# A decoder layer on one core: rows ahead of x, a later gate load, a first block by parts, rows used one place behind their loads, and wide products of ones

## The chip, the cores and the metric

The kernel runs on one core of a Trainium2 chip. The metric is the device time of one execution in microseconds (us). The core's engines run their own instruction streams: PE (TensorE, matmuls and transposes, with weight loads shown apart as PEld), DVE (VectorE), ACT (ScalarE), POOL (GpSimd) and SP (SyncE, which here only issues loads). Sixteen DMA engines move what SP, ACT and POOL issue.

## The reference

One hybrid decoder layer in float32, for 256 rows of width 2048. A conditioning vector `c` gives six rows of shifts, scales and gates by one matrix-vector product; the normalised and modulated `x` goes through a projection, two kinds of mixing heads, an output projection, and then a second normalisation and a gated feed-forward network.

```
c_act = silu(c)
mod = (c_act @ w_mod + b_mod)[:, None, :]            # w_mod: 2048 x 12288
sh_m, sc_m, g_m, sh_f, sc_f, g_f = split(mod, 6)
h = rmsnorm(x, mix_pre_w) * (1 + sc_m) + sh_m
proj = h @ w_in                                       # 2048 x 6160
cb, cc, cx, q, k, v, r, a_lr = split(proj, ...)       # a_lr: the last 16 columns
y_conv = cb * causal_dwconv3(cc * cx, conv_w)
log_a = log_sigmoid(a_lr @ gate_w2 + gate_b) / 16     # gate of the linear attention
o = rmsnorm(gla_chunked(q, k, v, log_a), gla_norm_w) * silu(r)
x = x + g_m * rmsnorm(concat(y_conv, o) @ w_out, mix_post_w)
h = rmsnorm(x, ffn_pre_w) * (1 + sc_f) + sh_f
u = causal_dwconv3(h @ w_up, ffn_conv_w)
g, val = split(u, 2)
x = x + g_f * rmsnorm((silu(g) * val) @ w_down, ffn_post_w)
```

## The kernel before

**Products in parts.** Each float32 matrix product is made of three faster ones: a weight tile is cast to a rounded type by ACT (`high`, line 140, tile `wh`), the remainder is taken by DVE (`low`, line 145, tile `wl`), and the activations are split likewise (`act_high`, `act_low`, line 380). A block adds high x high, high x low and low x high (lines 501 to 503).

**Units.** Work on PE is a list of units in a fixed order. A unit has `prep` (issue its weight load on SP, cast it on ACT), `low` (subtract on DVE), `mm` (its matmuls) and lists of other work at four places (`early`, `pre`, `mid`, `late`). `drive` walks the list: in unit i it runs `early`, then `prep` of unit i+2 and `low` of unit i+1, then `pre`, the matmuls, `mid` and `late`. All engines receive their instructions in this written order; what makes them wait is data and free buffers. Loaded tiles rotate through six `raw` buffers, `wh` and `wl` through three each, and most other tiles through twenty `big` buffers of one size (`slot`).

**Chunks.** The depth of the first projection (16 tiles of 128) is cut into `CHUNKS` of 2, 4, 5 and 5 tiles, with 12, 12, 16 and 18 units; then come 16 units of the output projection (`owait`), and the feed-forward part. Units of the first two chunks have four output tiles, those of the third three. A unit of the first chunk has 4 x 2 x 3 matmuls of 256 columns, one of the second 4 x 4 x 3, one of the third 3 x 5 x 3. In the list, unit 0 starts the first chunk, unit 12 the second, unit 24 the third, unit 40 the fourth.

**Modulation rows.** A chunk can only begin when its shift and scale are known. `mod_steps` computes them in 16 steps: step j loads the rows of `w_mod` that belong to c's j-th elements (SP) and adds them, times `c_act[:, j]`, to an accumulator over 128 partitions (DVE, line 136). For the chunks after the first these steps are spread over the `early` and `mid` places of the units given by `MODS`: units 0 to 9 for the second chunk, 10 to 20 for the third, 21 to 30 for the fourth, 31 to 43 for the gate row of the mixer, 44 to 67 for the first half of the feed-forward modulation. Then `mod_columns` sums the accumulator over the partitions and turns it into columns, by products with a matrix of ones of which 2 columns are used (line 282). Two units before a chunk ends (`LEAD`), the products for the next one stand in `early`, and in `late` the columns and the modulation of the activations (line 367); one unit later come the low parts and the products with the 16 gate columns `alr_w` (line 439), whose sum is taken in the next chunk's first unit (lines 447 and 449).

**The start.** For the first chunk the 16 steps stand ahead of everything. Four rows come in one load up to row 11, then two and two; the two halves of x (`load_x`) are issued after steps 0 and 8, and the norm of each (`NLD`, after steps 3 and 14) is computed as soon as it is written: squares on ACT (line 348), a sum on DVE (line 316), a root on ACT (line 318), a reciprocal on DVE (line 339), then the scaling of x, the first two tiles' columns on DVE (line 1028) and the rest on ACT (lines 1029 and 1030). After the rows SP loads `alr_w`, 16 columns of a wide matrix (line 1031). PE transposes x (line 361), sums the accumulator (line 282), and when the columns are there and the activations are modulated, cast and subtracted, it makes the gate products and begins unit 0. `drive` issues the first `prep`, `low` and second `prep` itself.

Of the kernel before, what the change touches and what calls it, by code (L numbers as in the profile page):

```python
# [14 lines left out]
P = 128  # L15
D = 2048
T = 256
# [19 lines left out]
XLD = (0, 8)  # L37
NLD = (3, 14)
# [3 lines left out]
MODS = (10, 21, 31, 44, 68)  # L42
# [7 lines left out]
NHF = 3  # L50

# [52 lines left out]
def layer_kernel(ctx: ExitStack, tc, x, c, w_mod, b_mod, mix_pre_w, mix_post_w, w_in, conv_w, gate_w2, gate_b,  # L104
# [47 lines left out]
    nc.scalar.activation(c_act, c_sb, AF.Silu)  # L152

# [3 lines left out]
    def mod_steps(s0, n, a, w, nj, first=False):  # L157

        accs, cur = [], {}

        def step(j):
            if j == 0:
                acc = cur["acc"] = (slot([P, n, w]) if n * w <= 1024 else
                                    wts.tile([P, n, w], F32, tag="macc", name=nm("macc"), bufs=2))
                accs.extend(acc[:, s, :] for s in range(n))
                if first:
                    cur["b"] = slot([1, n, w])
                    nc.gpsimd.dma_start(cur["b"], b_mod_v[:, s0:s0 + n, a:a + w])
                else:
                    nc.gpsimd.memset(acc, 0.0)  # L170
                    nc.gpsimd.dma_start(acc[0:1, :, :], b_mod_v[:, s0:s0 + n, a:a + w])
# [8 lines left out]
            src, cj = cur["r"][:, j % m, :, :], c_act[:, j:j + 1]  # L180
            if first and j == 0:
                nc.vector.tensor_scalar_mul(cur["acc"], src, cj)
            else:
                stt(cur["acc"], src, cj, cur["acc"])
            if first and j == 3:
                nc.vector.tensor_add(cur["acc"][0:1], cur["acc"][0:1], cur["b"])

        return accs, [lambda j=j: step(j) for j in range(KT)]

    accs0, steps0 = mod_steps(0, 2, 0, CHUNKS[0] * P, 4 if CHUNKS[0] < 3 else 2, True)  # L190

    ident = col(P, "ident")
    nc.scalar.dma_start(ident, ident_in)
# [3 lines left out]
    nc.scalar.copy(ones_r, ones)  # L197
    eps_t = col(1, "eps_t")
    nc.gpsimd.memset(eps_t, EPS)
# [69 lines left out]
    def mod_columns(accs, n, pre, tagname):  # L269

        ash = const.tile([P, 2 * n], F32, tag=tagname, name=nm("ash"))
        st = {}

        def products(tiles=None):
            r = ones if len(accs) == 2 else ones_r
            if "ps" not in st:
                st["ps"] = bank([P, 2 * n, 2])
            for o in (range(2 * n) if tiles is None else tiles):
                cs = slice((o % n) * P, (o % n + 1) * P)
                terms = (accs[o // n],) if len(accs) == 2 else accs[2 + o // n]  # L280
                for j, t in enumerate(terms):
                    nc.tensor.matmul(st["ps"][:, o, :], t[:, cs], r[:, 0:2], start=j == 0, stop=j == len(terms) - 1)  # L282

        def columns():
            nc.vector.tensor_copy(ash[:, :n], st["ps"][:, :n, 0])
            stt(ash[:, n:], st["ps"][:, n:, 0], 1.0, pre, ALU.add, ALU.mult)
# [134 lines left out]
    def modulate_chunk(ci, ash, early=None):  # L421
# [3 lines left out]

        def first():
            for kts in pairs(k0, k1):
                ps = early.pop(0) if early else turn_norm(xs, kts)
                hf = hf0[:, kts[0]:kts[-1] + 1, :] if ci == 0 else hf_tile()
# [5 lines left out]
        def second():  # L435
            ps = bank([P, T])
            for kts, hf, parts in kept:
                for i, k in enumerate(kts):
                    nc.tensor.matmul(ps[:16, :], alr_w[:, k, :], hf[:, i, :], start=(k == k0), stop=(k == k1 - 1))  # L439
                if parts:  # L440
                    act_low(*parts)
            kept.append(ps)

        def third():
            ps = kept.pop()
            if ci == 0:
                nc.vector.tensor_copy(alr[:16, :], ps[:16, :])
            else:
                nc.vector.tensor_add(alr[:16, :], alr[:16, :], ps[:16, :])

        return first, second, third

    def in_units(ci):
# [16 lines left out]
        def unit(tiles, plain):  # L470
# [3 lines left out]
            def prep():  # L474
                r = raw_tile([P, n, m * P])
# [9 lines left out]
            def mm():  # L485
                w = cur["w"]
                for o, nt in enumerate(tiles):
                    if nt // 2 not in banks:
                        more[nt // 2] = nt // 2 in left
                        banks[nt // 2] = left.pop(nt // 2) if more[nt // 2] else bank([P, 2, T])  # L490
# [874 lines left out]
```

## Time and profile before

| | |
|---|---|
| median of three runs | 1217.8 us (1215.99 to 1218.18) |
| the profiled execution | 1217.02 us |
| its span, first to last instruction | 1215.2 us |
| PE busy | 1177.5 us (97%) |
| DVE busy | 939.7 us (77%) |
| ACT busy | 570.0 us (47%) |
| HBM read | 315.42 MB |
| mean granted clock of PE | 0.996 |

A row of a group or of an engine's order gives the start and the duration, the engine, the line of the kernel, the operation, what is written from what is read with the shapes, and in brackets the idle time before it with what ended it. A run of equal instructions is merged into one row with their count; matmuls are pipelined, so the distance between starts, not the duration, is what one costs. A row of equal windows gives busy times of PE, PEld, DVE, ACT and POOL with the number of instructions, the granted clock of PE (1.00 is full), the mean busy share of the DMA engines, and GB/s.

### The profile page before, as it was taken

What the parts mean: (1) busy time and instruction counts of PE and PEld (TensorE: products, weight loads), DVE (VectorE), ACT (ScalarE), POOL (GpSimd) and SP (SyncE); (2) the same over time, 40 slices, a digit from 0 to 9 for tenths busy, and PEclk for the clock granted to TensorE, in tenths of its full rate; (3) what the DMA queues carried; (4) which work ended last, traced back from release to release, by engine and by line L of the source; (5) the groups of instructions that cost most, each with busy time, mean ns of one, the idle gap of its engine ahead of it and who ended that gap; (6) DMA issues with size and microseconds to landing.
All of it is one profiled execution on the core that took longest, in us unless ns stands there. A gap on an engine that the chain in (4) does not pass through costs nothing.

```text
span 1215.2 us, 17103 instructions
## 1 busy us (share of the span) xinstructions
PE 1177.5 (97%) x7003; PEld 1040.1 (86%) x7003; DVE 939.7 (77%) x955; ACT 570.0 (47%) x660; POOL 33.4 (3%) x52
## 2 busy tenths in 40 slices
PE   2999999999999999999999999999999999999997
PEld 1989999999997888888888888888888888888885
DVE  5989899999999886984598979698876664444463
ACT  5553423443474446444554545544544543443452
POOL 2000010000001001000000000000000000000000
PEclk9999999999999999999999999999999999999999
DMA  9999999986699886996666766767664665555522
GB/s 305 385 390 386 322 377 399 400 307 211 203 335 371 327 331 224 366 334 224 237 209 242 258 228 236 249 224 267 221 228 158 235 253 182 206 182 198 194 83 70
DMA packets 126735, 320.73 MB, mean 264 GB/s; under 512 B 8310, under 2 KB 34374, under 8 KB 116929
## 3 DMA queue, kind: packets, MB, share of 16 engines
q1 hardware_dynamic: 124048, 312.63, 72.1%
q0 software_dynamic: 2320, 6.94, 1.6%
q8 instruction: 55, 0.90, 0.3%
q14 instruction: 24, 0.19, 0.0%
q10 hardware_dynamic: 288, 0.07, 0.0%
HBM read 315.42 MB, written 4.19 MB: 263 GB/s over the span
## 4 chain that ended last, share of the span: by engine, by line
PE 92%; DMA 3%; DVE 2%; issue 1%; ACT 1%; SPq 0%; DVEq 0%; ACTq 0%
PE ps L912 27%; PE ps L914 14%; PE ps L768 9%; PE ps L769 9%; PE ps L770 9%; PE ps L501 6%; PE ps L502 6%; PE ps L503 6%; DMA raw<-in_w_mod_dram 3%; PE ps L600 1%; PE ps L498 1%; PE ps L282 1%; DVE wl L145 1%; DVE big L136 1%; PE ps L439 1%
## 5 line engine op out<-in xcount | busy, mean ns | idle before, releaser
L140 ACT CAST wh<-raw 128x2048 fp32r<-128x2048 f32 (+3 forms) x200 | 365.8, 1832 | 504.2 <-PE ps L912 195.0
L145 DVE TENSOR_TENSOR wl<-raw,wh 128x2048 fp32r<-128x2048 f32 (+3 forms) x200 | 437.0, 2187 | 142.8 <-ACT wh L140 142.8
L912 PE MATMUL ps<-big,wh 128*128 128x512 f32 x1400 | 494.8, 398 | 0.0
L914 PE MATMUL ps<-big,wl 128*128 128x256 f32 x1400 | 393.2, 281 | 1.1 <-DVE wl L145 1.1
L912 PEld LDWEIGHTS ps<-big,wh 128*128 128x128 f32 x1400 | 263.0, 188 | 64.7
L914 PEld LDWEIGHTS ps<-big,wl 128*128 128x128 f32 x1400 | 264.5, 189 | 1.5 <-DVE wl L145 1.5
L503 PE MATMUL ps<-big,wl 128*128 128x256 f32 x733 | 209.5, 286 | 2.7 <-DVE wl L145 2.6
L501 PE MATMUL ps<-big,wh 128*128 128x256 f32 x733 | 210.9, 288 | 0.2 <-ACT wh L140 0.2
L502 PE MATMUL ps<-big,wh 128*128 128x256 f32 x733 | 209.0, 285 | 0.3 <-DVE big L380 0.3
L136 DVE SCALAR_TENSOR_TENSOR macc<-raw,c_act,macc 128x2048 f32<-128x2048 f32 (+1 forms) x96 | 199.4, 2077 | 3.5 <-DMA raw<-in_w_mod_dram 3.4
L768 PE MATMUL ps<-wh,big 128*128 128x512 f32 x456 | 178.4, 391 | 0.0
L769 PE MATMUL ps<-wl,big 128*128 128x512 f32 x456 | 177.5, 389 | 0.0
L770 PE MATMUL ps<-wh,big 128*128 128x512 f32 x456 | 177.5, 389 | 0.0
L503 PEld LDWEIGHTS ps<-big,wl 128*128 128x128 f32 x733 | 142.1, 194 | 3.9 <-DVE wl L145 3.9
L501 PEld LDWEIGHTS ps<-big,wh 128*128 128x128 f32 x733 | 142.3, 194 | 2.7 <-ACT wh L140 1.4
L502 PEld LDWEIGHTS ps<-big,wh 128*128 128x128 f32 x733 | 142.3, 194 | 0.6 <-DVE big L380 0.5
L770 PEld LDWEIGHTS ps<-wh,big 128*128 128x128 f32 x456 | 85.6, 188 | 17.9
L768 PEld LDWEIGHTS ps<-wh,big 128*128 128x128 f32 x456 | 85.6, 188 | 17.9 <-issue 0.2
L769 PEld LDWEIGHTS ps<-wl,big 128*128 128x128 f32 x456 | 85.6, 188 | 17.7 <-issue 0.2
L136 DVE SCALAR_TENSOR_TENSOR big<-big,fcw,big 128x254 f32<-128x254 f32 (+1 forms) x176 | 72.1, 475 | 0.0
L838 DVE TENSOR_TENSOR big<-big,ps 128x256 f32<-128x256 f32 x88 | 31.1, 414 | 48.4 <-ACT big L836 48.4
L858 ACT ACTIVATE big<-big,fcw 128x256 f32<-128x256 f32 x88 | 37.9, 515 | 11.9 <-DVE big L849 11.9
(199 smaller groups left out, 665.8 us busy)
## 6 DMA issues: line engine op xcount, KB each, us to landing
raw<-in_w_up_dram SPq DMA_DIRECT2D x88, 1024.0 KB, 5.3
raw<-in_w_mod_dram SPq DMA_DIRECT2D x64, 1024.0 KB, 6.0
raw<-in_w_down_dram SPq DMA_DIRECT2D x44, 1024.0 KB, 4.8
raw<-in_w_in_dram SPq DMA_DIRECT2D x28, 960.0 KB, 8.1
raw<-in_w_mod_dram SPq DMA_DIRECT2D x32, 640.0 KB, 7.8
raw<-in_w_out_dram SPq DMA_DIRECT2D x16, 1024.0 KB, 6.5
raw<-in_w_in_dram SPq DMA_DIRECT2D x12, 1024.0 KB, 8.6
raw<-in_w_mod_dram SPq DMA_DIRECT2D x22, 512.0 KB, 6.6
```

Of the source, the lines that this page charges most:

```text
L136: nc.vector.scalar_tensor_tensor(o, a, s, b, op0=op0, op1=op1)
L140: nc.scalar.copy(hi, raw)
L145: nc.vector.tensor_sub(lo, raw, hi.bitcast(F32))
L501: nc.tensor.matmul(ps, w[0][:, kk, cs], ht[:, k % 2, 0, :], start=st, stop=False)
L502: nc.tensor.matmul(ps, w[0][:, kk, cs], ht[:, k % 2, 1, :], start=False, stop=False)
L503: nc.tensor.matmul(ps, w[1][:, kk, cs], ht[:, k % 2, 0, :], start=False, stop=sp)
L768: nc.tensor.matmul(ps, a[:, i, 0, ts_], w[0][:, kk, ns], start=st, stop=False)
L769: nc.tensor.matmul(ps, a[:, i, 0, ts_], w[1][:, kk, ns], start=False, stop=False)
L770: nc.tensor.matmul(ps, a[:, i, 1, ts_], w[0][:, kk, ns], start=False, stop=sp)
L858: nc.scalar.activation(st["c"][:, o, :], st["u"][o], AF.Copy, scale=fcw[:, 2, ch + o:ch + o + 1])
L912: nc.tensor.matmul(pss[o], wh[:, kk, cs], h2[k // 2][:, k % 2, :, :], start=(first and kk == 0), stop=False)
L914: nc.tensor.matmul(pss[o][:, 1, :], wl[:, kk, cs], h2[k // 2][:, k % 2, 0, :], start=False, stop=(last and kk == 3))
```

## The change

- **Start.** The rows of the first chunk are loaded first and used in a loop of their own (`first_load`, `first_step`). The halves of x are issued after the loads of rows 4 to 7 and 8 to 11. Rows 12 to 15 go to `big` buffers. The squares of x take two wide instructions a half instead of four; the root stands after step 9 or 13, and the reciprocal with the scaling of the first tiles one step later. The rest of x is scaled inside units 1 and 3 (`rest_of_rows`). The constant for the root is set by DVE, and a first root on ACT stands at the very beginning. The identity matrix is loaded by POOL's queue instead of ACT's.
- **Products of ones.** `keep_busy` puts 9, 1 and 3 products of 512 columns on PE, after the first transposes, after the second, and after the sums. In `mod_columns` the products with ones have 128 columns instead of 2, for every chunk and for the feed-forward modulation (the columns beyond the first are overwritten or unused).
- **First block.** The first weights' `prep` and `low` stand ahead of the columns. ACT writes the modulated high part directly, DVE computes the same value again for the low part (`at_once`). Unit 0 runs by parts: all high x high, then all low x high, then all high x low. The first four units' weights go to `big` buffers.
- **Gate.** `alr_w` is loaded in the third unit of the second chunk. The gate products of the first two chunks stand together in the second chunk's fifth unit, with the sum one unit later. For later chunks they stay where they were.
- **Rows.** For the second, third and fourth chunk a row is used one place after the place of its load (`lag`), seventeen steps in all. `MODS` and `CHUNK1` give: the second chunk's rows in units 0 to 9, the third's in 12 to 21, the fourth's in 24 to 31, the mixer's gate in 32 to 47, the feed-forward's in 48 to 67.

```diff
-XLD = (0, 8)
-NLD = (3, 14)
+XLD = (4, 8)
+NLD = (9, 13)
-MODS = (10, 21, 31, 44, 68)
+MODS = (10, 22, 32, 48, 68)
+CHUNK1 = 12
+BUSY = (9, 1, 3)
+WSLOT = 4
+GATE1 = 4
...
 def drive(units):
-    units[0].prep()
-    units[0].low()
-    units[1].prep()
...
+    eps_t = col(1, "eps_t")
+    nc.vector.memset(eps_t, EPS)
+    warm = col(1, "warm")
+    nc.scalar.activation(warm, eps_t, AF.Sqrt)
...
+    def mod_steps(s0, n, a, w, nj, lag=0):
+        accs, cur, rows = [], {}, []
+        def use(j, r):
+            stt(cur["acc"], r, c_act[:, j:j + 1], cur["acc"])
         def step(j):
+            if j >= KT:
+                use(*rows.pop(0))
+                return
...
+            rows.append((j, cur["r"][:, j % m, :, :]))
+            if j >= lag:
+                use(*rows.pop(0))
+        return accs, [lambda j=j: step(j) for j in range(KT + lag)]
...
-    nc.scalar.dma_start(ident, ident_in)
+    nc.gpsimd.dma_start(ident, ident_in)
+    nc.gpsimd.dma_start(first_b, b_mod_v[:, 0:2, 0:W0])
...
+    def keep_busy(n):
+        ps = bank([P, 4, P])
+        for i in range(n):
+            nc.tensor.matmul(ps, ones_r, busy_r, start=i == 0, stop=i == n - 1)
...
-                st["ps"] = bank([P, 2 * n, 2])
+                st["ps"] = bank([P, 4 * n + P])
...
-                    nc.tensor.matmul(st["ps"][:, o, :], t[:, cs], r[:, 0:2], ...)
+                    nc.tensor.matmul(st["ps"][:, 2 * o:2 * o + P], t[:, cs], r, ...)
...
+        def at_once():
+            n = CHUNKS[0]
+            for kts in pairs(k0, k1):
+                ps, hf = early.pop(0), hf0[:, kts[0]:kts[-1] + 1, :]
+                d = hts[kts[0] // 2] = slot([P, 2, 2, T], F32R)
+                ab = [(ash[:, n + k:n + k + 1], ash[:, k:k + 1]) for k in kts]
+                for i, (a, b) in enumerate(ab):
+                    nc.scalar.activation(d[:, i, 0, :], ps[:, i, :], AF.Identity, bias=b, scale=a)
+                for i, (a, b) in enumerate(ab):
+                    nc.vector.tensor_scalar(hf[:, i, :], ps[:, i, :], a, b, op0=ALU.mult, op1=ALU.add)
+                act_low(d, hf)
...
-                r = raw_tile([P, n, m * P])
+                r = slot([P, n, m * P]) if ci == 0 and tiles[0] < 4 * WSLOT else raw_tile([P, n, m * P])
...
+                if by_parts:
+                    for j, (wi, xl) in enumerate(((0, 0), (1, 0), (0, 1))):
+                        for kk in range(n):
+                            for o, nt in enumerate(tiles):
+                                nc.tensor.matmul(banks[nt // 2][:, nt % 2, :], w[wi][:, kk, o * P:(o + 1) * P],
+                                                 hts[(k0 + kk) // 2][:, (k0 + kk) % 2, xl, :], ...)
...
+    for j in range(0, 12, 4):
+        first_load(j, 4, raw_tile)
         if j in XLD:
             load_x(XLD.index(j))
+    for j in range(12, KT, 2):
+        first_load(j, 2, slot)
+    load_small()
...
+    ss = halves_squared(0)
+    for j in range(KT):
+        first_step(j)
+        if j == 7:
+            small_columns()
         if j in NLD:
             t = NLD.index(j)
+            rs[t] = std_of(ss, 2, f"n1{t}")
+            if t == 0:
+                ss = halves_squared(1)
+        if j - 1 in NLD:
+            norm_rows(NLD.index(j - 1))
-    nc.sync.dma_start(alr_w, ...)
     early = [turn_norm(xs, kts, None, (0,)) for kts in pairs(0, CHUNKS[0])]
+    keep_busy(BUSY[0])
     for kts, ps in zip(pairs(0, CHUNKS[0]), early):
         turn_norm(xs, kts, ps, (1,))
+    keep_busy(BUSY[1])
     ash, products, columns = mod_columns(...)
     products()
+    keep_busy(BUSY[2])
+    chunks[0][0].prep()
+    chunks[0][0].low()
     columns()
+    first, second = modulate_chunk(0, ash, early)
+    first()
+    second()
+    chunks[0][1].prep()
+    chunks[1][2].early.append(lambda: nc.sync.dma_start(alr_w, ...))
+    chunks[0][1].late.append(lambda: rest_of_rows(0))
+    chunks[0][3].late.append(lambda: rest_of_rows(1))
...
-        st["accs"], steps = mod_steps(0, 2, bounds[ci] * P, n * P, 2 if n <= 4 else 1)
-        spread(steps, allin[at:MODS[ci - 1]])
+        st["accs"], steps = mod_steps(0, 2, bounds[ci] * P, n * P, 2 if n <= 4 else 1, 1)
+        spread(steps, allin[max(at, CHUNK1 * (ci - 1)):MODS[ci - 1]])
...
+        seconds.append((us[-LEAD + 1].late if ci > 1 else chunks[1][GATE1].mid, gate_products))
+        seconds.append((chunks[ci][0 if ci > 1 else GATE1 + 1].mid, gate_sum))
```

More of the change, by code (lines that the diff above doesn't have):

```diff
@@ L179, in step, with first_load, first_step @@
                         nc.sync.dma_start(cur["r"][:, :, s, :], w_mod_v[:, j:j + m, s0 + s, a:a + w])
[L180 to L190, printed above, removed]
+            rows.append((j, cur["r"][:, j % m, :, :]))
+            if j >= lag:
+                use(*rows.pop(0))
+        return accs, [lambda j=j: step(j) for j in range(KT + lag)]
+    W0 = CHUNKS[0] * P
+    first_acc = slot([P, 2, W0])
+    first_b = slot([1, 2, W0])
+    first_rows = {}
+    def first_load(j, m, tile):
+        r = tile([P, m, 2, W0])
+        for s in range(2):
+            nc.sync.dma_start(r[:, :, s, :], w_mod_v[:, j:j + m, s, 0:W0])
+        for i in range(m):
+            first_rows[j + i] = r[:, i, :, :]
+    def first_step(j):
+        cj = c_act[:, j:j + 1]
+        if j == 0:
+            nc.vector.tensor_scalar_mul(first_acc, first_rows[j], cj)
+        else:
+            stt(first_acc, first_rows[j], cj, first_acc)
+        if j == 3:
+            nc.vector.tensor_add(first_acc[0:1], first_acc[0:1], first_b)
     ident = col(P, "ident")
-    nc.scalar.dma_start(ident, ident_in)
+    nc.gpsimd.dma_start(ident, ident_in)
+    nc.gpsimd.dma_start(first_b, b_mod_v[:, 0:2, 0:W0])
     ones = col(P, "ones")
@@ L435, in second, with gate_products, gate_sum @@
         def second():
-            ps = bank([P, T])
             for kts, hf, parts in kept:
-                for i, k in enumerate(kts):
-                    nc.tensor.matmul(ps[:16, :], alr_w[:, k, :], hf[:, i, :], start=(k == k0), stop=(k == k1 - 1))
                 if parts:
                     act_low(*parts)
[L442 to L451, printed above, removed]
+                for i, k in enumerate(kts):
+                    gate_terms.append((k, hf[:, i, :]))
+        return first, second
+    gate_terms, gate_ps = [], []
+    def gate_products():
+        ps = bank([P, T])
+        for i, (k, h) in enumerate(gate_terms):
+            nc.tensor.matmul(ps[:16, :], alr_w[:, k, :], h, start=i == 0, stop=i == len(gate_terms) - 1)
+        gate_ps.append((ps, gate_terms[0][0] == 0))
+        gate_terms.clear()
+    def gate_sum():
+        ps, is_first = gate_ps.pop(0)
+        if is_first:
+            nc.vector.tensor_copy(alr[:16, :], ps[:16, :])
+        else:
+            nc.vector.tensor_add(alr[:16, :], alr[:16, :], ps[:16, :])
     def in_units(ci):
@@ L468, in in_units, with unit @@
         banks, done, begun, more = {}, {}, {}, {}
-        def unit(tiles, plain):
+        def unit(tiles, plain, by_parts=False):
             m = len(tiles)
@@ L514, in unit @@
             return Unit(prep, lows, mm, [fin])
-        return [unit(g, i in (PLAIN, FULL1, FULL2, FULL)[ci]) for i, g in enumerate(groups)]
+        return [unit(g, i in (PLAIN, FULL1, FULL2, FULL)[ci], ci == 0 and i == 0) for i, g in enumerate(groups)]
     mts = {}
@@ L1015, in down_unit, with halves_squared @@
         return Unit(prep, lows, mm, [fin] if k == NK - 1 else [])
-    for j, f in enumerate(steps0):
-        f()
+    for j in range(0, 12, 4):
+        first_load(j, 4, raw_tile)
         if j in XLD:
             load_x(XLD.index(j))
-        if j == 0:
-            load_small()
+    for j in range(12, KT, 2):
+        first_load(j, 2, slot)
+    load_small()
+    chunks = [in_units(ci) for ci in range(len(CHUNKS))]
+    e = CHUNKS[0] * P
+    rs = {}
+    def halves_squared(t):
+        ss, jk = small.tile([P, 4], F32, tag=f"n1{t}ss", name=nm("ss")), slot([P, 1024])
+        for h in range(2):
+            nc.scalar.activation(jk, xs[t][h], AF.Square, accum_out=ss[:, h:h + 1])
+        return ss
```

64 lines of the change are left out of this document (32 added, 32 removed).

## The prediction

> **What bounds the kernel now.** I read the page first, then busy time in equal windows, then each engine's order of instructions in the first 80 us.
>
> ```profile
> span 1215.2 us, 17103 instructions
> PE 1177.5 (97%) x7003; PEld 1040.1 (86%) x7003; DVE 939.7 (77%) x955; ACT 570.0 (47%) x660; POOL 33.4 (3%) x52
> ...
> 0.00:20.00 20.00, 1.01 (x3) 0.46 (x3) 10.40 (x16) 10.70 (x22) 8.65 (x23) 1.00 0.93 313
> 20.00:40.00 20.00, 14.19 (x76) 11.94 (x77) 15.27 (x22) 10.89 (x17) 0.00 (x0) 1.00 1.00 339
> 40.00:60.00 20.00, 18.68 (x152) 18.08 (x151) 17.07 (x15) 11.29 (x17) 0.00 (x0) 1.00 1.04 381
> 60.00:80.00 20.00, 18.75 (x146) 16.91 (x145) 18.11 (x16) 12.67 (x17) 0.00 (x0) 1.00 1.05 391
> ...
> 180.00:200.00 20.00, 20.00 (x169) 20.00 (x168) 20.00 (x14) 5.97 (x4) 0.00 (x0) 1.00 1.03 398
> ```
>
> A window's columns are PE, PEld, DVE, ACT and POOL busy, the granted clock, the DMA share and GB/s. PE is idle for 37.7 of 1215.2 us, and 27.4 of these lie before 80 us. From there to the end PE hardly stops, so a microsecond by which PE reaches the second chunk earlier is a microsecond of the end, unless a later stage takes it back. The DMA engines are full from 40 us on (1.04 and 1.05) at 381 to 398 GB/s. The opening is therefore a race between PE and the loads.
>
> The start, as the order of DVE and PE shows it:
>
> ```profile
> 23.72 0.75 DVE L136 SCALAR_TENSOR_TENSOR big<-raw,c_act,big 128x512 f32<-128x512 f32 x1
> ...
> 24.61 1.84 PE L282 MATMUL ps<-ones,big 128*128 128x2 f32 x8
> ...
> 29.47 0.58 PE L501 MATMUL ps<-big,wh 128*128 128x256 f32 x1 [0.17 <-ACT wh L140]
> ...
> 31.01 0.58 PE L503 MATMUL ps<-big,wl 128*128 128x256 f32 x1 [0.74 <-DVE wl L145]
> ...
> 34.38 0.41 PE L503 MATMUL ps<-big,wl 128*128 128x256 f32 x1
> 34.59 0.41 PE L501 MATMUL ps<-big,wh 128*128 128x256 f32 x1
> ...
> 35.13 0.28 PE L501 MATMUL ps<-big,wh 128*128 128x256 f32 x1
> 35.25 0.27 PE L502 MATMUL ps<-big,wh 128*128 128x256 f32 x1
> ```
>
> The last modulation row is done at 24.47, the first block begins at 29.47 and can go on only at 31.01. Until about 35 us matmuls start 0.21 us apart, then 0.12 apart: PE begins at half rate. A unit of the first chunk has 24 matmuls, 2.87 us at 0.1195.
>
> Where that race ends:
>
> ```profile
> 57.87 2.61 DVE L136 SCALAR_TENSOR_TENSOR big<-raw,c_act,big 128x1024 f32<-128x1024 f32 x2 [0.63 <-DMA raw<-in_w_mod_dram]
> 60.39 1.22 DVE L145 TENSOR_TENSOR wl<-raw,wh 128x1024 fp32r<-128x1024 f32 x1
> 61.94 2.61 DVE L136 SCALAR_TENSOR_TENSOR big<-raw,c_act,big 128x1024 f32<-128x1024 f32 x2 [0.33 <-DMA raw<-in_w_mod_dram]
> ...
> 64.80 1.92 PE L282 MATMUL ps<-ones,big 128*128 128x2 f32 x16 [0.25 <-PE ps L503]
> ...
> 73.38 1.90 PE L439 MATMUL ps<-hf,alr_w 128*16 128x256 f32 x8
> 75.21 0.39 PE L501 MATMUL ps<-big,wh 128*128 128x256 f32 x1
> 75.90 0.39 PE L502 MATMUL ps<-big,wh 128*128 128x256 f32 x1 [0.31 <-DVE big L380]
> ```
>
> The last two modulation rows of the second chunk are waited for until 61.94, DVE spends 2.52 on them (57.87 to 60.39 for a pair), and the products that need them start at 64.80, at the head of the eleventh unit. This landing sets the time, not the start of PE.
>
> **The change, part by part.** I price everything by when those products start, and by what follows.
>
> *The gate load, moved.* It stands ahead of the first weights on SP.
>
> ```profile
> 20.00:24.00 4.00, 0.14 (x1) 0.15 (x2) 3.21 (x8) 1.28 (x4) 0.00 (x0) 1.00 0.85 170
> ...
> DMA packets 3150, 1.38 MB, mean 229 GB/s; under 512 B 2126, under 2 KB 2960, under 8 KB 3150
> ...
> alr_w<-in_w_in_dram SPq DMA_DIRECT2D x1, 128.0 KB, 7.8
> raw<-in_w_in_dram SPq DMA_DIRECT2D x12, 512.0 KB, 7.4
> ...
> raw<-in_w_mod_dram SPq DMA_DIRECT2D x32, 640.0 KB, 7.8
> ...
> raw<-in_w_in_dram SPq DMA_DIRECT2D x28, 960.0 KB, 8.1
> ```
>
> The packets are those of 18 to 24 us: two thirds are under 512 B, and 20 to 24 moves 170 GB/s where its neighbours move about 385. That is 4 x (385 - 170) / 385 = 2.23 us, gained by everything behind it. The load returns in the third unit of the second chunk, where the products wait for nothing else: that chunk loads sixteen rows of 640 KB and twelve weight tiles of 1024 KB (twice those of 512) in twelve units of 48 matmuls (5.74 us) and 2.7 of gate products, 322 GB/s, so it is hidden; without that slack it costs the 2.23 again.
>
> *Rows of the second chunk.* Seventeen steps in the same twenty places instead of sixteen: the last pair is loaded half a unit earlier, so one weight tile of 512 KB moves behind it on SP, 0.524 MB / 385 = 1.36 us. Using rows one place behind holds each buffer half a unit longer; the first four weight tiles go to other buffers, which pays for that here. The landing becomes 61.94 - 2.23 - 1.36 = 58.35, and with 2.52 of DVE the products start at 60.9. The queue moved 381 GB/s from 40 to 60 us, so little more is in it. From the other side, DVE: sixteen rows at 1.26 and ten low parts at 1.22 are 32.4 us, from the first low part of the activations at about 26.5 (an estimate: the last row two rows' time earlier than 24.47 because DVE no longer stands waiting for a root, then 1.8 of products and 2 of columns, modulation and subtraction) to 58.9. So 58.9 to 60.9, the landing row being the nearer, so 60.5: a gain of 4.3 (3.9 to 5.9).
>
> *The start itself* (rows before x, the square-root table loaded early, the row scales split, the cast of the first weights ahead of the columns, the first block by parts, nine, one and three 512-wide products of ones to warm PE): worth zero at the end, to my reading. Even if the block could still only go on at 31.01, ten warm units of 2.87 end at 59.7, before 60.5. The loads are the cover. If they came sooner, the start would decide: up to 5 us more. The nine products of ones stand ahead of the second transposes on PE's queue: 512 columns cold are twice 0.21, 3.8 us in all, beside DVE's last rows, so some tenths at worst and under the same cover. `ident` goes from ACT's queue to POOL's; behind it there stand the small rows and the next accumulators' memsets, none needed before the fourth row. DVE's copies of ones run before its first load has landed. `rest_of_rows` adds four copies to ACT, which is busy 11.29 of 20 in this chunk: hidden.
>
> *The second chunk's entry.* From 64.80 PE has products, two units, transposes and the gate products, then a stall of 0.57 (75.33 became 75.90). The third chunk's rows are gone from DVE here, but so is the cover of the gate products (1.83), under which ACT modulates behind this cast:
>
> ```profile
> 68.15 1.90 ACT L140 CAST wh<-raw 128x2048 fp32r<-128x2048 f32 x1 [2.34 <-DMA raw<-in_w_in_dram]
> ```
>
> The cast waits for a tile that comes two tiles behind the last rows. Between no stall and 0.57 + 1.83, I take 0.4, as the rows freed on DVE are worth about what the cover was: +0.2 (-1.8 to +0.6).
>
> *Gate products together.* Twelve of 0.229 (1.83 / 8) in the second chunk instead of eight there and four in the start: 4 x 0.23 = -0.9, on PE's path.
>
> *Wide products of ones.*
>
> ```profile
> 226.36 2.29 PE L282 MATMUL ps<-ones,macc 128*128 128x2 f32 x20
> 228.51 0.36 PE L501 MATMUL ps<-big,wh 128*128 128x256 f32 x1
> ...
> 230.00:232.00 2.00, 2.00 (x11) 2.00 (x11) 2.00 (x4) 0.00 (x0) 0.00 (x0) 0.50 1.04 413
> ...
> 466.76 1.05 PE L1216 MATMUL ps<-big,big 128*128 128x128 f32 x8
> 467.57 0.48 PE L912 MATMUL ps<-big,wh 128*128 128x512 f32 x1
> ```
>
> A product with 2 columns takes 0.1075 (2.15 / 20), one of the same type with 128 columns 0.101 (0.81 / 8): the width is free (bounds for 120 of them: -0.8 to 0.8). And about a microsecond after the twenty narrow ones the granted clock is 0.50; from 229.6 to 232.9 sixteen matmuls stand 0.213 apart, as the cold ones of the start do, 16 x (0.213 - 0.1195) = 1.5 us. I take that as theirs and as gone: +1.5 (0 to 1.5; below nothing if the twelve gate products, with 16 of 128 columns of weights, make a dip of their own).
> The Trainium skill, "TensorE: Matmul & The Clock Gate", in "Why this matters for your kernels", asks only for no idle gap of about 3 us between bursts; here none existed, and the clock fell nevertheless. By that rule the dip would not be the narrow products' and would stay, and the sum would lose its 1.5.
>
> *Later rows.* The third chunk's rows leave the last two units of the first chunk for ten of the second's. The fourth's 16 fall into 8 units instead of 10, the next 16 into 16 instead of 13, the last 16 into 20 instead of 24.
>
> ```profile
> 158.43 2.15 DVE L145 TENSOR_TENSOR wl<-raw,wh 128x1920 fp32r<-128x1920 f32 x1
> 160.50 1.54 DVE L136 SCALAR_TENSOR_TENSOR macc<-raw,c_act,macc 128x1280 f32<-128x1280 f32 x1
> 161.96 1.27 DVE L419 TENSOR_TENSOR big<-big,ps 128x512 f32<-128x512 f32 x2
> 163.16 1.54 DVE L136 SCALAR_TENSOR_TENSOR macc<-raw,c_act,macc 128x1280 f32<-128x1280 f32 x1
> ...
> 188.30 2.35 DVE L136 SCALAR_TENSOR_TENSOR macc<-raw,c_act,macc 128x2048 f32<-128x2048 f32 x1
> 190.56 0.68 DVE L419 TENSOR_TENSOR big<-big,ps 128x512 f32<-128x512 f32 x1
> ```
>
> In those eight units DVE has a low part 2.07, two rows of 1.46 and 1.5 additions of 0.6: 5.89 us against 45 matmuls, 5.38. Eight times 0.51 is 4.1 us behind. Before, nine units had 1.23 rows of 2.26, 5.75 us, 3.3 behind in all, and PE was busy 20.00 of 20.00. So 3.3 is known to be covered by the buffers; I take 0 and keep 0 to 4.1.
>
> Sum: 4.3 + 0.2 - 0.9 + 1.5 = 5.1 us. The profiled execution took 1217.02 (span 1215.2 and 1.8 around it), 0.8 below the median of 1217.8; I subtract from the median: 1212.7.
>
> **Rivals.**
> *The loads do not hold it.* If DVE, or PE from a block started near 25.5 (a microsecond ahead of the subtraction at 26.5), sets the products (58.9, or 25.5 + 28.7 = 54.2), the gain is 1.6 to 6.3 more: 1211.1 to 1206.4. Against it: the landing at 61.94 and full DMA engines.
> *The dip stays, or another comes:* 1214.2. For it: of the runs of narrow products only this one is followed by a slow stretch, so something else may have made it. This is also what the rule of the Trainium skill above gives.
> *The dense fourth-chunk rows take the gain back.* With no cover, 4.1 us: 1216.8, no change.
> *Slower.* The same eight units have three tiles each in six raw buffers. A weight tile is held for some 8 us of landing (8.1 for the 960 KB tiles), 1.8 of cast (1.90 x 1920 / 2048) and 2.07 of low part, and rows are now held half a unit (2.7) longer. Six buffers over a mean hold of 12 to 12.8 us give three tiles in 6.0 to 6.4 us, against 5.38. At 6.4, 8 x 1.02 = 8.2 is lost: 1220.9. It eats the gain at 6.02 and makes the kernel measurably slower above 6.3. Against it: SP starts these rows two units ahead, and the nine dense units before ran without a stall.
>
> **How the numbers follow.** A change of 0.2%, 2.4 us, is about what a measurement here can tell from none. Forecast 0.53; loads not holding 0.15; dip 0.14 (still faster by over 0.2%, save at the bad end of its terms); gain taken back 0.11; slower 0.07. Faster 0.80, the same 0.13, slower 0.07. The forecast's own range is 1210.5 to 1214.5. From 1208.3 to 1217.0 leaves out the early PE start and the slower case.
>
> **What would show it.** The sixteen products of the second chunk near 60.5, with DVE's rows before them still ended by a load; 20 to 24 us near 385 GB/s; the first block near 25.5, at 0.12 us spacing; no window with clock 0.50 near 222; PE busy 20.00 in the windows from 140 to 240. Wrong, if the products start before 58 or after 63, if PE waits for `wl` in the third chunk, or if a dip follows the gate products.

## The result and the profile after

| | before | after |
|---|---|---|
| median | 1216.85 us (14 runs, 1215.03 to 1220.29) | 1220.03 us (14 runs, 1219.54 to 1221.41) |
| ratio | | 1.0027, 95% interval 1.0019 to 1.0034 |
| profiled execution | 1217.02, span 1215.2 | 1220.02, span 1218.2 |

The kernel became slower by 0.27%. The prediction was 1212.7 us, faster; its range ended at 1217.0.

The page of the kernel after, and equal windows of its span (columns as before: PE, PEld, DVE, ACT, POOL busy, granted clock, DMA share, GB/s):

```profile
span 1218.2 us, 17123 instructions
PE 1180.1 (97%) x7016; PEld 1041.0 (85%) x7016; DVE 941.5 (77%) x959; ACT 567.8 (47%) x651; POOL 35.7 (3%) x52
...
20.00:24.00 4.00, 4.00 (x12) 2.84 (x10) 3.38 (x7) 1.45 (x4) 0.00 (x0) 1.00 1.05 384
...
60.00:80.00 20.00, 20.00 (x169) 19.87 (x168) 15.42 (x13) 15.38 (x19) 0.00 (x0) 1.00 1.00 341
...
140.00:240.00 100.00, 100.00 (x818) 96.98 (x817) 95.77 (x73) 38.73 (x31) 10.69 (x7) 1.00 0.98 366
...
340.00:360.00 20.00, 16.13 (x122) 15.10 (x121) 18.75 (x23) 17.01 (x35) 0.37 (x1) 0.98 0.95 345
360.00:380.00 20.00, 20.00 (x89) 16.34 (x88) 20.00 (x17) 10.38 (x9) 0.84 (x1) 0.93 0.96 344
400.00:420.00 20.00, 18.70 (x82) 15.13 (x82) 15.52 (x10) 9.66 (x13) 0.00 (x0) 1.00 0.93 354
```

Up to 240 us these windows are what was forecast: 384 GB/s where there were 170, no stall behind 60 us, PE busy 100.00 of 100.00 at clock 1.00. Then PE loses 3.87 us between 340 and 360, runs at a mean clock of 0.93 up to 380, and loses 1.30 more between 400 and 420.

PE's order in the kernel after, at the heads of its stages (start, duration, line, what; in brackets the idle time before):

```profile
26.53 1.22 PE L554 MATMUL ps<-big,wh 128*128 128x256 f32 x8 [0.28 <-ACT big L468]
...
60.59 2.01 PE L316 MATMUL ps<-ones,big 128*128 128x128 f32 x16
...
129.70 2.40 PE L316 MATMUL ps<-ones,macc 128*128 128x128 f32 x20
...
222.58 2.40 PE L316 MATMUL ps<-ones,macc 128*128 128x128 f32 x20
...
333.77 1.89 PE L771 MATMUL ps<-big,big 128*128 128x256 f32 x8
...
350.74 0.38 PE L572 MATMUL ps<-big,wl 128*128 128x256 f32 x1 [0.45 <-DVE wl L146]
...
354.19 0.60 PE L801 MATMUL ps<-ident,big 128*128 128x128 f32 x4
354.99 0.49 PE L837 MATMUL ps<-wh,big 128*128 128x512 f32 x1 [0.20 <-ACT wh L141]
358.70 0.50 PE L838 MATMUL ps<-wl,big 128*128 128x512 f32 x1 [3.21 <-DVE wl L146]
...
360.09 0.63 PE L839 MATMUL ps<-wh,big 128*128 128x512 f32 x1
360.51 0.63 PE L837 MATMUL ps<-wh,big 128*128 128x512 f32 x1
...
365.66 0.60 PE L801 MATMUL ps<-ident,big 128*128 128x128 f32 x4
...
402.18 0.50 PE L838 MATMUL ps<-wl,big 128*128 128x512 f32 x1 [1.30 <-DVE wl L146]
```

and the same places of the kernel before that the prediction doesn't show:

```profile
133.48 2.29 PE L282 MATMUL ps<-ones,macc 128*128 128x2 f32 x20
...
338.92 1.89 PE L702 MATMUL ps<-big,big 128*128 128x256 f32 x8
...
358.49 0.60 PE L732 MATMUL ps<-ident,big 128*128 128x128 f32 x4
358.85 0.48 PE L768 MATMUL ps<-wh,big 128*128 128x512 f32 x1
359.17 0.49 PE L769 MATMUL ps<-wl,big 128*128 128x512 f32 x1
...
364.51 0.60 PE L732 MATMUL ps<-ident,big 128*128 128x128 f32 x4
```

Subtracting place by place gives PE's lead over the kernel before: 4.21 us at the second chunk's products (64.80 to 60.59), 3.78 at the third's, 3.78 at the fourth's, 5.15 at the last mixing heads (338.92 to 333.77), 4.30 at the transposes ahead of the output projection. The forecast was 4.3, then 5.1 at the end of the sum. At the first unit of the output projection PE then waits 3.21 us for `wl`, DVE's low part of that unit's weights. From about 359.5 its matmuls stand 0.42 apart (360.09 to 360.51, at a granted clock of 0.50 from 360 to 362) where the kernel before has 0.23. One unit later the lead has become a lag of 1.15 (364.51 to 365.66). The wait at 402 takes 1.30 more, and the spans differ by 3.0.

Why `wl` is late stands in DVE's order and groups. Kernel before, and then kernel after (a group's row: line, operation, shapes and count, then busy time and mean ns of one, then idle time before; the windows run from 238 to 359 us before and from 233 to 358 after, some units 40 to 57 in each):

```profile
246.15 0.40 DVE L449 TENSOR_TENSOR alr<-alr,ps 16x256 f32<-16x256 f32 x1
...
356.81 2.29 DVE L145 TENSOR_TENSOR wl<-raw,wh 128x2048 fp32r<-128x2048 f32 x1
359.02 2.35 DVE L136 SCALAR_TENSOR_TENSOR macc<-raw,c_act,macc 128x2048 f32<-128x2048 f32 x1
...
L136 DVE SCALAR_TENSOR_TENSOR macc<-raw,c_act,macc 128x2048 f32<-128x2048 f32 x13 | 30.4, 2342 | 0.0
```

```profile
239.80 0.40 DVE L510 TENSOR_TENSOR alr<-alr,ps 16x256 f32<-16x256 f32 x1
...
356.36 2.28 DVE L146 TENSOR_TENSOR wl<-raw,wh 128x2048 fp32r<-128x2048 f32 x1
...
L137 DVE SCALAR_TENSOR_TENSOR macc<-raw,c_act,macc 128x2048 f32<-128x2048 f32 x16 | 37.5, 2344 | 0.0
```

In the kernel before this low part ends at 359.10 (356.81 + 2.29) and PE takes it at 359.17: it is just in time, with no slack to speak of. In the kernel after, DVE is 6.35 us ahead at the gate sum of the fourth chunk (246.15 to 239.80) and only 0.45 ahead at this low part (356.81 to 356.36). Between them lie 16 wide modulation rows instead of 13. They take 7.1 us more (37.5 - 30.4; 6.8 by the distance between starts, 2.26). DVE loses 5.9 of its lead and not 6.8, mostly because its gaps between these two places shrink as well (4.7 us before, 4.0 after, most of them waits for ACT and PE). PE arrives 4.3 ahead and finds its data 0.45 ahead.

### The profile page after: what moved, and what is told of

Its sections match the earlier page's. It is cut to its first block, busy times and chain, and to the rows that moved or that the text cites. A ratio compares the mean times of both kernels' runs of the same rounds, so it can differ in the third digit from the quotient of the medians.

```text
span 1218.2 us, 17123 instructions
## 1 busy us (share of the span) xinstructions
PE 1180.1 (97%) x7016; PEld 1041.0 (85%) x7016; DVE 941.5 (77%) x959; ACT 567.8 (47%) x651; POOL 35.7 (3%) x52
## 4 chain that ended last, share of the span: by engine, by line
PE 85%; DVE 9%; DMA 3%; issue 2%; ACT 1%; SPq 1%; DVEq 0%; ACTq 0%
PE ps L981 27%; PE ps L983 13%; PE ps L838 9%; PE ps L839 9%; PE ps L837 9%; PE ps L572 5%; PE ps L570 5%; PE ps L571 5%; DVE macc L137 2%; DVE wl L146 2%; DMA raw<-in_w_mod_dram 2%; PE ps L316 1%; DVE big L137 1%; DMA big<-in_w_mod_dram 1%; DVE big L453 1%
## 5 line engine op out<-in xcount | busy, mean ns | idle before, releaser
L141 ACT CAST wh<-raw 128x2048 fp32r<-128x2048 f32 (+3 forms) x196 | 361.6, 1847 | 497.8 <-PE ps L981 191.8
L146 DVE TENSOR_TENSOR wl<-raw,wh 128x2048 fp32r<-128x2048 f32 (+3 forms) x196 | 432.2, 2207 | 145.0 <-ACT wh L141 145.0
L981 PEld LDWEIGHTS ps<-big,wh 128*128 128x128 f32 x1400 | 263.0, 188 | 64.9
L570 PE MATMUL ps<-big,wh 128*128 128x256 f32 x725 | 206.8, 285 | 0.0
L571 PE MATMUL ps<-big,wh 128*128 128x256 f32 x725 | 205.2, 283 | 0.0
L570 PEld LDWEIGHTS ps<-big,wh 128*128 128x128 f32 x725 | 139.0, 192 | 1.7 <-issue 1.3
L571 PEld LDWEIGHTS ps<-big,wh 128*128 128x128 f32 x725 | 139.0, 192 | 0.2
```

The source lines that it names most:

```text
L141: nc.scalar.copy(hi, raw)
L146: nc.vector.tensor_sub(lo, raw, hi.bitcast(F32))
L570: nc.tensor.matmul(ps, w[0][:, kk, cs], ht[:, k % 2, 0, :], start=st, stop=False)
L571: nc.tensor.matmul(ps, w[0][:, kk, cs], ht[:, k % 2, 1, :], start=False, stop=False)
L981: nc.tensor.matmul(pss[o], wh[:, kk, cs], h2[k // 2][:, k % 2, :, :], start=(first and kk == 0), stop=False)
```

## Experiments

Theory A: the rows that the change moved late (mixer's gate to units 32 to 47, feed-forward to 48 to 67) put three more wide rows into units 40 to 57, where DVE has little time free, and PE waits for DVE. Rivals: B, the fourth chunk's rows packed into eight units push DVE back; C, it is the load or the cast behind `wl`; D, the new start costs something later. The kernel before ran beside each group, with medians of 1217.03, 1216.68 and 1216.49 us in the first three and 1216.68 beside the last run.

**The new start with rows earlier.** Kernel after, with

```diff
-MODS = (10, 22, 32, 48, 68)
-CHUNK1 = 12
+MODS = (10, 22, 31, 44, 68)
+CHUNK1 = 11
```

> The changed kernel with the row places of before from the fourth chunk on: the fourth chunk's rows in units 22 to 30, the mixer's gate rows in 31 to 43, the feed-forward rows in 44 to 67; the third chunk's in 11 to 21. Theory A (the later places put three more 2048-wide rows, 3 x 2.26 = 6.8 us, into the stretch of units 40 to 57 where DVE is full): the lead of 5 us that PE has at the mixing heads' output products stays to the end, about 1212 us, and PE waits under 0.5 us for the first output unit's low part. Theory B (DVE is full in that stretch with any placing, so it takes whatever lead PE brings): 1215.5 to 1217, and the wait stays at 2 us or more. Theory C (the wait is for a load or a cast, not for DVE's rows): 1219 to 1220.

Measured 1211.89 us (5 runs, 1210.24 to 1212.51), ratio 0.9949, interval 0.9935 to 0.9963. PE's and DVE's order at the first output unit:

```profile
354.00 0.49 PE L838 MATMUL ps<-wl,big 128*128 128x512 f32 x1
...
351.65 2.29 DVE L146 TENSOR_TENSOR wl<-raw,wh 128x2048 fp32r<-128x2048 f32 x1
353.86 2.35 DVE L137 SCALAR_TENSOR_TENSOR macc<-raw,c_act,macc 128x2048 f32<-128x2048 f32 x1
```

The wait is gone, and the low part is again ready just in time (it ends at 353.94, PE takes it at 354.00). By the medians the places of the later rows cost 8.1 us, and D falls: the rest of the change is worth 5.1, the sum that was forecast. (The quotient of the medians is 0.9958; the ratio 0.9949 would give 6.2, its interval 4.5 to 7.9.)

**The old start with the rows late.** Kernel before, with

```diff
-MODS = (10, 21, 31, 44, 68)
+MODS = (10, 22, 32, 48, 68)
+CHUNK1 = 12
...
-        spread(steps, allin[at:MODS[ci - 1]])
+        spread(steps, allin[max(at, CHUNK1 * (ci - 1)):MODS[ci - 1]])
```

> The kernel before with only the row places of the changed one (third chunk 12 to 21, fourth 24 to 31, gate rows 32 to 47, feed-forward rows 48 to 67). Theory A: the low part of the first output unit, which came just in time at 359.0, comes some 5 us later, PE stalls, its clock falls: 1222 to 1225 us. Theory B: no lead, so nothing to take: 1216.5 to 1218. Theory C: as B.

Measured 1225.09 us (5 runs, 1222.91 to 1225.54), ratio 1.0058, interval 1.0045 to 1.0070. PE's order, and DVE's:

```profile
363.23 0.79 PE L770 MATMUL ps<-wl,big 128*128 128x512 f32 x1 [3.22 <-DVE wl L146]
...
360.89 2.28 DVE L146 TENSOR_TENSOR wl<-raw,wh 128x2048 fp32r<-128x2048 f32 x1
```

The same wait appears in a kernel that has nothing else of the change, and costs 8.1 us there too, 0.1 above the upper end of what A gave. The halves are additive: against the kernel before that ran beside them they are -5.14 and +8.06, together +2.92, and the whole change measured +3.18.

**The feed-forward rows loaded, but hardly added.** Kernel after, with 64 of 1024 columns of each of these rows added and the rest of that modulation left out:

```diff
-    f1, fsteps = mod_steps(3, 2, 0, 1024, 1)
+    f1, fsteps = mod_steps(3, 2, 0, 1024, 1, 0, 64)
```

> The changed kernel in which the feed-forward rows of units 48 to 67 are loaded as before but only 64 of each 1024 columns are added (that part of the modulation is left out). Eight rows of 2.26 us go from DVE in units 48 to 57. Theories A and B: the wait of 3.2 us before the first output unit goes, and so do the slow clock after it and the wait near 402; 1211.5 to 1213. Theory C: the wait stays, 1219 to 1220.

Measured 1211.62 us (4 runs, 1211.46 to 1211.81), ratio 0.9951, interval 0.9938 to 0.9965. The loads and the casts are as in the kernel after and only DVE's work is smaller, and the waits for `wl` at the output projection are gone from PE's list of waits. C falls; it is DVE's time.

**The wait filled with matmuls.** Kernel after, with 14 products of ones ahead of the first output unit's:

```diff
+                    for _ in range(14 if nh == 0 else 0):
+                        nc.tensor.matmul(pss[0, 0], ones_r, cur["w"][0][:, 0, 0:512], start=True, stop=True)
```

> The changed kernel with 14 products of ones (512 columns, 0.227 us each, 3.2 us) ahead of the first output unit's blocks, where PE would stand waiting. If the slow matmuls after the wait (nine to ten at 0.43 instead of 0.227, some 1.9 us) come from the wait itself, the clock stays full and the time is 1218 to 1218.5. If they have another cause, 1220.

Measured 1218.63 us (10 runs, 1218.30 to 1219.14), ratio 1.0013, interval 1.0004 to 1.0022; PE's order:

```profile
355.34 3.54 PE L864 MATMUL ps<-wh,ones_r 128*128 128x512 f32 x14 [0.21 <-ACT wh L141]
358.72 0.39 PE L837 MATMUL ps<-wh,big 128*128 128x512 f32 x1
359.05 0.50 PE L838 MATMUL ps<-wl,big 128*128 128x512 f32 x1
359.38 0.40 PE L839 MATMUL ps<-wh,big 128*128 128x512 f32 x1
```

The unit begins no earlier than in the kernel after (359.05 against 358.70), but at full rate, and 1.4 us come back (1220.03 to 1218.63). The ranges of the two kernels don't overlap. So the wait's after-effect on the clock was about 1.4 of the loss. The Trainium skill, "TensorE: Matmul & The Clock Gate", in "What's actually happening", has the clock fall to half after an idle window of about 3.4 us. The wait of 3.21 us here is slightly shorter than that and was followed by the 0.42 spacing; the one of 1.30 at 402 was not, with clock 1.00 in its window.

The next seven change one thing (the last of them two) in the kernel of the first experiment, the base (1211.89). They ran beside other runs of the kernel before, and the intervals of most overlap with the base's, so differences under some 1.5 us are read from the traces as well, by two places on PE:

| | second chunk's products | last mixing heads | median |
|---|---|---|---|
| base | 60.36 | 333.75 | 1211.89 |
| narrow products of ones | 60.50 | 335.24 | 1213.32 |
| no products for the clock | 60.65 | 333.78 | 1212.19 |
| gate load early | 63.70 | 337.16 | 1215.12 |
| rows used at their load's place | 61.48 | 335.27 | 1213.87 |
| x after the first four rows | 61.34 | 334.57 | 1212.95 |
| two plain units | 59.76 | 333.56 | 1212.49 |
| two plain units, rows to unit 71 | 60.13 | 333.10 | 1211.33 |

One trace scatters too: five kernels that are alike up to the second chunk's products (the base, the kernel after, and three others of it, with hardly added rows, with the wait filled and with only the fourth chunk dense) have them between 60.36 and 60.93. A difference under 0.6 in that column is no reading.

**Narrow products of ones again.** Two columns instead of 128:

```diff
-                    nc.tensor.matmul(st["ps"][:, 2 * o:2 * o + P], t[:, cs], r, ...)
+                    nc.tensor.matmul(st["ps"][:, 2 * o:2 * o + 2], t[:, cs], r[:, 0:2], ...)
```

> The changed kernel with the old places (1211.9 us), and the products with ones 2 columns wide again in every chunk. Theory 1 (a run of twenty narrow products lets the clock fall, where it lies inside one period of the clock's control): a window with granted clock 0.50 near 130 or near 222 in some executions, 0 to 1.5 us slower, 1212 to 1213.4. Theory 2 (the slow stretch before had another cause; the width costs or saves nothing): 1211.9 and no such window.

Measured 1213.32 us (5 runs, 1212.40 to 1213.54), ratio 0.9967, interval 0.9954 to 0.9979: 1.4 above the base by the medians, 1.49 by the heads. PE's order and windows:

```profile
129.62 2.29 PE L316 MATMUL ps<-ones,macc 128*128 128x2 f32 x20
...
132.00:134.00 2.00, 2.00 (x13) 2.00 (x13) 2.00 (x4) 0.00 (x0) 0.00 (x0) 0.61 0.86 295
134.00:136.00 2.00, 2.00 (x12) 2.00 (x12) 2.00 (x2) 0.00 (x0) 0.00 (x0) 0.54 0.67 190
```

The dip is back, behind the third chunk's products this time and not behind the fourth's (clock 1.00 from 222 to 234 us). It isn't one execution's: all five have a mean clock of 0.996 or 0.997, all five of the base 0.998. The kernel with the old start and the rows late, whose products are narrow as in the kernel before, has the dip as well, behind its fourth chunk's products (225.63):

```profile
230.00:232.00 2.00, 2.00 (x12) 2.00 (x11) 2.00 (x5) 0.00 (x0) 0.00 (x0) 0.50 1.04 411
```

So all three traces with narrow products have one dip, and no trace with wide ones has any there. The narrow products make it, and which of the runs is hit changes from kernel to kernel.

**No products of ones for the clock.** The three calls of `keep_busy` left out:

```diff
-    keep_busy(BUSY[0])
...
-    keep_busy(BUSY[1])
...
-    keep_busy(BUSY[2])
```

> The changed kernel with the old places, without the thirteen products of ones that keep PE busy in the start. Theory 1 (the loads set when the second chunk's products start, so PE's clock in the first block is covered): the first block starts with matmuls 0.21 us apart, the sixteen products stay at 60.4, 1211.9 us. Theory 2 (the start of PE counts): the products come 2 us later, 1214.

Measured 1212.19 us (5 runs, 1211.89 to 1212.60), ratio 0.9960, interval 0.9947 to 0.9972, no measurable difference. PE's order:

```profile
26.71 2.08 PE L554 MATMUL ps<-big,wh 128*128 128x256 f32 x8 [0.98 <-ACT big L468]
...
60.65 2.00 PE L316 MATMUL ps<-ones,big 128*128 128x128 f32 x16
```

The first block now starts at half rate (2.08 us for the first eight matmuls, 1.22 in the kernel after). The second chunk's products come 0.29 later, which is within the scatter, and the heads 0.03. The warm start is hidden.

**The gate load early again.**

```diff
+    nc.sync.dma_start(alr_w, w_in[:, 6144:6160].rearrange("(k p) n -> p k n", p=P))
...
-    chunks[1][2].early.append(lambda: nc.sync.dma_start(alr_w, ...))
```

> The changed kernel with the old places, with only the load of the gate's 16 columns back ahead of the first weights on SP. Theory 1 (its small packets cost the queue 2.2 us, and the loads set the second chunk's products): 20 to 24 us near 170 GB/s, the sixteen products at 62.5, 1214 us. Theory 2 (another engine sets them): products at 60.4, 1211.9.

Measured 1215.12 us (11 runs, 1213.45 to 1216.19), ratio 0.9985, interval 0.9976 to 0.9993: 3.2 above the base. A window, and PE's order:

```profile
20.00:24.00 4.00, 4.00 (x12) 2.82 (x10) 3.41 (x7) 0.59 (x3) 0.00 (x0) 1.00 0.83 148
...
63.70 2.01 PE L316 MATMUL ps<-ones,big 128*128 128x128 f32 x16
```

The load is worth 3.2 to 3.4 (60.36 to 63.70, 333.75 to 337.16), more than the 2.23 that the prediction took; at 148 GB/s the window gives 4 x (385 - 148) / 385 = 2.5, and where the rest comes from was not separated.

**Rows used at their load's place, and x issued after the first four rows.** The first hunk is the one kernel, the second the other:

```diff
-        st["accs"], steps = mod_steps(0, 2, bounds[ci] * P, n * P, 2 if n <= 4 else 1, 1)
+        st["accs"], steps = mod_steps(0, 2, bounds[ci] * P, n * P, 2 if n <= 4 else 1, 0)
...
-XLD = (4, 8)
+XLD = (0, 8)
```

> The changed kernel with the old places, with the rows of the second to fourth chunk used at the place of their load (sixteen steps instead of seventeen). Theory 1 (the last pair is loaded half a unit later, behind one more weight tile of 512 KB, and DVE stands in its order before each row that has not landed): products 1.4 us later or a little more, 61.8 to 62.5, 1213.3 to 1214. Theory 2 (DVE's amount of work sets them): 60.4, 1211.9.

> The changed kernel with the old places, with the first half of x loaded ahead of rows 4 to 7 again. The start is covered by what DVE and the loads do up to 60.4: DVE gets its second group of rows 1.05 MB later (2.7 us), has 3 us to wait in the start, and makes up part of it while x waits for its norm. If only what lies after the start counts, 1211.9 (1211.5 to 1212.4); if DVE's chain of work counts from the start on, up to 2 us more, 1213 to 1214.

Measured 1213.87 us (8 runs, 1213.51 to 1214.99; 0.9972, 0.9962 to 0.9983) and 1212.95 us (8 runs, 1210.76 to 1213.18; 0.9970, 0.9960 to 0.9980): 2.0 and 1.1 above the base by the medians, 1.5 and 0.8 by the heads. DVE's group of rows in units of the first chunk (28 to 60 us), from the run with `lag` 0:

```profile
L137 DVE SCALAR_TENSOR_TENSOR big<-raw,c_act,big 128x1024 f32<-128x1024 f32 x16 | 20.5, 1282 | 2.8 <-DMA raw<-in_w_mod_dram 2.6
```

DVE waits 2.6 us for loads there, and 1.6 in the base kernel. For the rows, theory 1's time holds, and the products came somewhat earlier than it gave. The order in which x and the rows come was priced at zero; by the two places and the medians it is worth about 1, though the intervals of the times overlap.

**Two plain units.** Units 5 and 7 of the first chunk take one product of unsplit weights each, which spares DVE two low parts (2.4 us); then the same with the feed-forward rows spread up to unit 71:

```diff
-PLAIN = ()
+PLAIN = (5, 7)
```

```diff
-MODS = (10, 22, 31, 44, 68)
+MODS = (10, 22, 31, 44, 72)
-F2_AT = (68, 73, 16)
+F2_AT = (72, 73, 16)
```

> The changed kernel with the old places (1211.9 us), with units 5 and 7 of the first chunk as plain float32 products: no cast and no low part for them (2.4 us less on DVE, 2 us less on ACT), 0.8 us more on PE for each. Theory DVE (DVE's sixteen rows and eleven low parts set the second chunk's products, with 1.5 us of waits for loads): products 1 to 2 us earlier than 60.4, 1210 to 1211. Theory loads (the last pair of rows lands too late for more): products at 60.0 to 60.4, 1211.5 to 1212. If the extra PE time were not covered: 1213.5.

> As plain_two, and the feed-forward rows are spread over units 44 to 71 instead of 44 to 67 (the next ones start at 72): 1.3 rows of 2.26 us, 3 us, leave DVE in units 44 to 57. If DVE there, whose low part for the first output unit is just in time, eats what plain_two brings, this one is 1 to 2 us faster than plain_two; if not, the two agree within 0.5 us.

Measured 1212.49 us (7 runs, 1211.83 to 1213.53; 0.9968, 0.9957 to 0.9980) and 1211.33 us (5 runs, 1211.20 to 1212.07; 0.9961, 0.9949 to 0.9974). With 2.4 us of DVE's work taken away the products start at 59.76 and 60.13, 0.6 and 0.2 before the base's, and DVE's waits for loads rise to 3.2 and 3.4. The first kernel meets the numbers of neither theory. The two units also take PE 0.8 us more (3.26 for one, start to start, where a unit in parts takes 2.87), so DVE's work, the loads and PE's own time aren't separated by this. Neither kernel is separable from 1211.89. The second is 1.2 below the first, as expected if DVE ate the gain later, but their intervals overlap and their heads differ by 0.46, so that isn't shown. It has the fastest median of the kernels that leave nothing out, by 0.6, and its interval overlaps with that of the first experiment.

**Only the fourth chunk's rows dense.** Kernel after, with the gate rows in units 32 to 43 and the feed-forward's in 44 to 67:

```diff
-MODS = (10, 22, 32, 48, 68)
+MODS = (10, 22, 32, 44, 68)
```

> The kernel after, with the mixer's gate rows in units 32 to 43 and the feed-forward rows in units 44 to 67; the fourth chunk's sixteen rows stay in the eight units 24 to 31, as in the kernel after. This separates the two parts of the later rows. Theory A (what is lost is lost by the 16 instead of 13 rows in units 40 to 57, and nothing in units 24 to 31): the wait for `wl` at the first output unit is gone or under 0.5 us, products of the fourth chunk near 222.6, 1211.5 to 1213. Theory B (the eight dense units push DVE's work behind, and the first output unit pays for it): the wait stays at 1 us or more, 1215 to 1219.

Measured 1216.65 us (11 runs, 1216.23 to 1216.86), ratio 0.9998, interval 0.9989 to 1.0007. The expectation from A fails here. Windows and PE's order:

```profile
140.00:240.00 100.00, 97.33 (x799) 95.13 (x798) 96.86 (x72) 35.57 (x30) 7.46 (x4) 1.00 0.98 369
...
208.63 0.39 PE L572 MATMUL ps<-big,wl 128*128 128x256 f32 x1 [1.54 <-DVE wl L146]
...
234.75 0.35 PE L570 MATMUL ps<-big,wh 128*128 128x256 f32 x1 [1.06 <-DVE big L453]
...
358.53 0.50 PE L838 MATMUL ps<-wl,big 128*128 128x512 f32 x1 [0.95 <-DVE wl L146]
```

PE loses 2.67 us before 240, nearly all of it in two waits for DVE (1.54 for a low part, 1.06 for an addition), where both the kernel after and that of the first experiment have 100.00 of 100.00. By the prediction's durations (low part 2.07, additions 0.9, a unit of PE 5.38) the dense units 24 to 31 leave DVE 4.1 behind in this kernel and in the kernel after alike. What differs is what follows: here 1.33 wide rows a unit (2.07 + 0.9 + 1.33 x 2.26 = 5.98), eight times 0.60 or 4.8 more behind, 8.9 in all; in the kernel after one row a unit (5.23), and 1.2 recovered. In the first experiment the sum is 7 x 0.19 + 9 x 0.37 = 4.6 (units 24 to 30 with 16/9 rows of 1.46, then 31 to 39 with 16/13 of 2.26), which PE didn't feel. So by this estimate a backlog of 4.6 is covered and one of 8.9 is not; by the 2.67 lost, some 6.2 were. The sums leave out that DVE also waits for row loads between 130 and 245 us, 2.0 here and 1.4 in the other two.

B's time thus holds for this kernel, though most of its loss falls earlier than at the first output unit (0.95), and A holds for the kernel after: it is one mechanism. DVE's rows must be added somewhere between 140 and 360 us, DVE has hardly a gap there, and where they stand thickest for long enough PE waits. The 16-unit stretch for the gate rows spared the fourth chunk and pushed the surplus to the output projection.

## Why the prediction was wrong, point by point

- *Later rows.* This is the step that failed. It priced units 24 to 31 alone, found 0 to 4.1 and took 0. There the reading was right: PE busy 100.00 from 140 to 240. But the same paragraph names "the next 16 into 16 instead of 13, the last 16 into 20 instead of 24" and gives these no price. Counted over units 40 to 57, they are 16 rows for 13, 6.8 us of DVE in a stretch whose low part for the first output unit ended 0.07 us before its use. Measured, the term is -8.1: by the trace some 3.9 of lead that DVE no longer had (0.45 and 3.21 of waiting, with 0.2 for the cast), about 1.4 of clock, 1.3 at 402, and the remaining 1.5 not itemised. "3.3 is known to be covered" was a statement on units 31 to 39 of the kernel before and was carried to other stages.
- *Rivals.* "The dense fourth-chunk rows take the gain back" had the right engine and the wrong units. The slower one forecast 1220.9, near the result, by a shortage of raw buffers in units 24 to 31; PE doesn't wait there, so its number is chance.
- *Second chunk.* Products at 60.5 forecast, 60.59 measured. The mechanism is only half right: the last rows are no longer ended by a load.

```profile
57.73 2.60 DVE L137 SCALAR_TENSOR_TENSOR big<-raw,c_act,big 128x1024 f32<-128x1024 f32 x2
...
L137 DVE SCALAR_TENSOR_TENSOR big<-raw,c_act,big 128x1024 f32<-128x1024 f32 x16 | 20.5, 1281 | 1.7 <-DMA raw<-in_w_mod_dram 1.5
```

  In DVE's order of the kernel after, the last pair has no bracket, and in 28 to 62 us all waits for loads are 1.5. The prediction's bound of DVE's work (58.9) with these 1.5 gives 60.4. But PE also comes out of the tenth unit without a gap (busy 8.59 of 8.59 us from 52.00 to 60.59), 0.26 after the rows end at 60.33, and had waited 3.4 us for DVE's low parts before 52: the low parts may set the products as much as the rows. A microsecond more of waits for loads moved them 1.1 later. That 60.5 was met to 0.1 is in part luck: put back one at a time, the gate load, the lag and the order of x moved the products by 3.3, 1.1 and 1.0, where the prediction has 2.2, 1.4 and nothing.
- *Gate load.* 2.2 forecast, 3.2 to 3.4 measured by putting it back.
- *The start itself.* Zero forecast. For the warm products it holds (0.03 at the heads); for the order of x it is about 1, not clear of the noise in the times.
- *Second chunk's entry and gate products.* +0.2 and -0.9, together -0.7; the lead goes from 4.21 to 3.78 at the third chunk, -0.4. The stall of 0.57 is gone altogether.
- *Wide products of ones.* +1.5 forecast, 1.4 measured, and the lead grows by 1.37 from the fourth chunk's products to the heads (3.78 to 5.15). The rule of the Trainium skill cited in the prediction, by which the dip would have stayed, is not borne out: no gap stood ahead of the dips, and they went with the width.
- *The sum up to the output projection.* 5.1 forecast, 5.15 measured at 333.77, and 5.1 in the first experiment's median.

## What to carry to other kernels

When work is moved along a full engine, add up its backlog over every stage from the move to the end, not at the densest one alone: count rows of a kind between two milestones in both kernels. Before a gain on the bounding engine is carried to the end, look for the places where its data is ready just in time (ready time against use time), since there the lead counts only as far as the supplying engine has the same lead. Changes that come as a package are worth splitting: here one part was worth 5.1 us, the other -8.1, and the version without the second part beats both kernels (ratio 0.9949).

## What was not expected of the hardware

Twenty products of 2 columns, back to back and with PE counted busy, can be followed by some 3.3 us at half clock (229.6 to 232.9 us before, 132.4 to 135.7 in the run with narrow ones, 229.2 to 232.5 with the old start and the rows late); products of 128 columns take the same time (2.16 us for twenty, 222.58 to 224.74) and none of the kernels that have them shows it. Only one of the runs of narrow products is hit in each of the three traces, and not always the same one. The scatter of the kernel before may come from this: of its 62 executions beside the experiments, the nine with a mean clock of 0.998 or 0.999 took 1214.9 to 1215.6 us, the 21 with 0.994 or 0.995 took 1216.3 to 1218.9. One dip lowers the mean by 0.0014 (an estimate: half of 3.3 in 1215 us), so these would be executions with none and with about two; that isn't shown, as only one execution of this kernel was traced (0.996, one dip). The Trainium skill, "TensorE: Matmul & The Clock Gate", in "What's actually happening", speaks of a free-running window of activity of about 3.4 us: the length agrees, and if narrow products count as little activity the changing place would follow, but no run here shows what is counted.
